# Moving every input and output buffer of a transpose kernel to a multiple of 256 bytes in its SBUF partition

## The chip, the cores and the metric

The kernel runs on one core of one Trainium2 chip. The metric is the device time in microseconds (us) of one execution. Several executions of each kernel were timed, and the median is quoted with the range. The span is the time from the first to the last instruction of the profiled execution. HBM is the memory outside the core, SBUF the core's own buffer memory, cut into 128 partitions, and PSUM the memory into which TensorE writes.

## The reference

```python
# x: 8192 x 8192 float32
def reference(x):
    return np.transpose(x)
```

The kernel has to read 268 MB from HBM, transpose, and write 268 MB back.

## The kernel before

The kernel works in blocks of 1024 rows by 2048 columns. Two loads bring a block into an input buffer. TensorE transposes it in tiles of 128 by 128 against an identity matrix, ScalarE and VectorE take turns in copying the results from PSUM into output buffers, and each full output buffer is stored. There are 64 loads of 4 MB and 128 stores of 2 MB.

```python
    R = 8
    C = 16
    I = R * P            # 1024
    J = C * P            # 2048
    G = 4
    LS = 2

    const_pool = ctx.enter_context(tc.tile_pool(name="const", bufs=1))
    in_pool = ctx.enter_context(tc.tile_pool(name="in_pool", bufs=2))
    out_pool = ctx.enter_context(tc.tile_pool(name="out_pool", bufs=4))
    # ... psum pool
    ident = const_pool.tile([P, P], dt)
    make_identity(nc, ident)
    # ... for each block:
            in_tile = in_pool.tile([P, R, J], dt)
            rs = R // LS
            for s in range(LS):
                src = x[i0 + s * rs * P:i0 + (s + 1) * rs * P, j0:j0 + J]
                src = src.rearrange("(a p) j -> p a j", p=P)
                nc.sync.dma_start(out=in_tile[:, s * rs:(s + 1) * rs, :], in_=src)
            for g in range(C // G):
                out_tile = out_pool.tile([P, G, I], dt)
                # ... transposes into PSUM, copies into out_tile
                dst = out[j0 + g * G * P:j0 + (g + 1) * G * P, i0:i0 + I]
                dst = dst.rearrange("(b q) i -> q b i", q=P)
                nc.scalar.dma_start(out=dst, in_=out_tile)
```

The contiguous runs are 8192 bytes for a load (`J` floats) and 4096 bytes for a store (`I` floats). Each is one DMA packet. The pools are laid out one after another in a partition. In the built program 16 KB of scratch, 128 bytes of constants and the 512-byte identity come first, so the input buffers start at bytes 17024 and 82560 and the output buffers from 148096 on. All of these are 128 past a multiple of 256. The sizes of the buffers are multiples of 256, so every packet in them starts at 128 past one as well.

## Time and profile before

| | before |
|---|---|
| time, median (range) | 1279.2 us (1277.5 to 1279.7) |
| DMA rate over the span | 421 GB/s |
| TensorE, VectorE, ScalarE busy | 55%, 25%, 20% |

These lines are from the page of the kernel before. The first gives busy time per engine with its share of the span. The next two cut the span in 40 slices: busy tenths of the 16 DMA engines, and the rate. Then come the two data queues, stores (q10) and loads (q1), with packets, MB, and the time that their packets took as a share of 16 engines' span. The last is the chain of work that ended last.

```profile
PE 700.7 (55%) x4096; PEld 629.0 (49%) x4096; DVE 313.5 (25%) x256; ACT 252.8 (20%) x257; POOL 0.7 (0%) x6
...
DMA  9999999999999999999999999999999999999999
GB/s 392 425 423 424 425 423 425 423 422 424 423 422 423 424 424 423 424 422 423 424 424 422 422 422 424 424 423 423 423 423 424 422 422 422 424 424 423 422 422 375
...
q10 hardware_dynamic: 67584, 268.44, 51.4%
q1 hardware_dynamic: 33792, 268.44, 49.8%
...
DMA out_dram<-out_tile 87%; PE ps L63 6%; DVE out_tile L71 3%; DMA in_tile<-in_x_dram 2%; ACT out_tile L69 0%; DVEq L71 0%; ACTq L69 0%; SPq L55 0%
```

No compute engine is near full. The DMA engines are busy from the first slice to the last, and the rate is flat. The chain is stores for 87% of the span. The kernel is bound by DMA, so what a packet costs should move its time.

Two stretches of the same trace, from the view of busy time by window. The columns are: window and length in us, then busy us (and instructions) of PE, PEld, DVE, ACT and POOL, the clock granted to TensorE, the DMA share and the rate in GB/s. In the first window only loads run; in the second both directions do, apart from short pauses of the loads.

```profile
14.00:28.00 14.00, 7.81 (x40) 7.40 (x39) 2.45 (x2) 2.06 (x3) 0.00 (x0) 0.76 1.02 424
...
100.00:600.00 500.00, 277.85 (x1600) 249.21 (x1600) 122.14 (x101) 97.72 (x100) 0.00 (x0) 0.73 1.02 423
```

The trace also has a record of every DMA packet. 31618 of 32768 load packets last exactly 309 ns, and 64265 of 65536 store packets exactly 159 ns.

### The profile page before, as it was taken

Reading aid. Unit: us, or ns where it says so; the run is one execution under the profiler, and the core shown is the slowest. Engines: PE = TensorE matmul, PEld = TensorE weight load, DVE = VectorE, ACT = ScalarE, POOL = GpSimd, SP = SyncE. Lnnn points to the kernel's source line nnn. Section 1 sums busy time; section 2 is a strip of 40 time slices with the busy share of each in tenths; the row PEclk is TensorE's granted clock in tenths of the full one; section 3 lists DMA queues with packets and bytes.
Section 4 is the critical chain, followed back from the end, with each engine's and each line's share of the span. In section 5 each row is a group of like instructions: output and inputs, shape, how many; then the busy total and the mean of one; then the engine's idle time right before and its main releaser. Section 6 shows DMA issues by size and latency. Waiting matters only on the chain.

```text
span 1276.3 us, 9511 instructions
## 1 busy us (share of the span) xinstructions
PE 700.7 (55%) x4096; PEld 629.0 (49%) x4096; DVE 313.5 (25%) x256; ACT 252.8 (20%) x257; POOL 0.7 (0%) x6
## 2 busy tenths in 40 slices
PE   3555555655565545655556555555555655556463
PEld 3454455544554544544445554454444544445453
DVE  1222223222232222322123221222222322122222
ACT  1221112121121211212112121221211212112121
POOL 0000000000000000000000000000000000000000
PEclk8777777767777677776677766878667777677867
DMA  9999999999999999999999999999999999999999
GB/s 392 425 423 424 425 423 425 423 422 424 423 422 423 424 424 423 424 422 423 424 424 422 422 422 424 424 423 423 423 423 424 422 422 422 424 424 423 422 422 375
DMA packets 101418, 537.49 MB, mean 421 GB/s; under 512 B 3072, under 2 KB 3072, under 8 KB 68608
## 3 DMA queue, kind: packets, MB, share of 16 engines
q10 hardware_dynamic: 67584, 268.44, 51.4%
q1 hardware_dynamic: 33792, 268.44, 49.8%
q8 instruction: 32, 0.52, 0.1%
q14 instruction: 10, 0.08, 0.0%
HBM read 268.44 MB, written 268.44 MB: 421 GB/s over the span
## 4 chain that ended last, share of the span: by engine, by line
DMA 89%; PE 6%; DVE 3%; issue 0%; ACT 0%; DVEq 0%; ACTq 0%; SPq 0%
DMA out_dram<-out_tile 87%; PE ps L63 6%; DVE out_tile L71 3%; DMA in_tile<-in_x_dram 2%; ACT out_tile L69 0%; DVEq L71 0%; ACTq L69 0%; SPq L55 0%
## 5 line engine op out<-in xcount | busy, mean ns | idle before, releaser
L63 PE MATMUL ps<-ident,in_tile 128*128 128x128 f32 x4096 | 700.7, 344 | 560.5 <-DVE out_tile L71 535.3
L63 PEld LDWEIGHTS ps<-ident,in_tile 128*128 128x128 f32 x4096 | 629.0, 181 | 631.9 <-DVE out_tile L71 605.9
L71 DVE COPY out_tile<-ps 128x1024 f32<-128x1024 f32 x256 | 313.5, 1225 | 948.9 <-DMA out_dram<-out_tile 593.7
L69 ACT COPY out_tile<-ps 128x1024 f32<-128x1024 f32 x256 | 251.5, 1014 | 1007.1 <-DMA out_dram<-out_tile 832.2
L69 ACT ACT_TABLE_LOAD x1 | 1.3, 1283 | 0.7 <-PEq L91 0.7
masks.py:199 POOL TENSOR_SCALAR_AFFINE_SELECT ident<-ident 128x128 f32<-128x128 f32 x1 | 0.3, 292 | 0.1
masks.py:197 POOL MEMSET ident<- 128x128 f32 x1 | 0.2, 204 | 0.3 <-POOLq L91 0.3
L91 POOL MEMSET const-bfloat16-1.0<- 128x1 bf16 x1 | 0.1, 101 | 0.0
L91 POOL MEMSET const-uint8-127<- 128x1 uint8 x1 | 0.1, 101 | 0.0
L91 POOL MEMSET const-float32-0.0<- 128x1 f32 x1 | 0.1, 98 | 0.2 <-issue 0.2
L91 POOL MEMSET const-float32-1.0<- 128x1 f32 x1 | 0.1, 98 | 0.0
## 6 DMA issues: line engine op xcount, KB each, us to landing
in_tile<-in_x_dram SPq DMA_DIRECT2D x64, 4096.0 KB, 27.9
out_dram<-out_tile ACTq DMA_DIRECT2D x128, 2048.0 KB, 28.9
```

The lines of the kernel that those rows point to most:

```text
L63: nc.tensor.transpose(ps[:, a * P:(a + 1) * P], in_tile[:, a, b * P:(b + 1) * P], ident,)
L69: nc.scalar.copy(out=out_tile[:, bb, :], in_=ps)
L71: nc.vector.tensor_copy(out=out_tile[:, bb, :], in_=ps)
L91: nc = _bacc.Bacc("TRN2", target_bir_lowering=False, num_devices=1)
```

## The change

The intent is that every DMA packet begins at a multiple of 256 bytes in its partition. A tile of 128 bytes is put in front of the identity. The buffers then start at 17152, 82688, 148224 and so on, which are all multiples of 256.

```diff
+    pad = const_pool.tile([P, 32], dt)
+    nc.gpsimd.memset(pad, 0.0)
     ident = const_pool.tile([P, P], dt)
     make_identity(nc, ident)
```

Nothing else changes. The instruction streams of all engines are the same in order, but for one more memset on GpSimd.

## The prediction

> **What bounds the kernel now.** The 16 DMA engines. In the 40-slice view they are 90% busy or more throughout and move 422 to 425 GB/s in every slice but the first and last; 537 MB at 421 GB/s over the span. TensorE is busy 55%, VectorE 25%, ScalarE 20%. The chain that ended last is 89% DMA, nearly all stores. Their waits for stores (594 and 832 us) stand behind full queues. Only what makes a DMA packet cheaper moves the time.
>
> **What the change does.** Built, the buffers before start at byte 17024 (input) and 148096 (output) of a partition, all at 128 past a multiple of 256. The 128-byte pad puts all on a multiple. Packets stay 8 KB (loads) and 4 KB (stores), HBM addresses stay. Instruction order is the same but for one more GpSimd memset; the one on the identity took 0.2 us, long before the first load lands at about 13 us. It costs nothing.
>
> **What it could be worth.** The Trainium skill, "DMA: Bandwidth & Descriptors", section "How a descriptor splits into AXI transactions", says that a transaction starts at a multiple of 256 bytes and unused bytes before the start still cost 32-byte beats: here 4, so 132 for 128 in a store, and 260 for 256 in a load if writes pay too. Estimates:
> - both sides pay, exposed: 12 beats of 524 per load packet and two store packets, 2.3%: about 1250 us;
> - only reads (stores) pay: 8 of 520: about 1260 us;
> - hidden behind a fixed cost per packet but for one cycle: about 1271 us;
> - not exposed: 1279 us.
>
> **What the trace says of it.** Nearly all load packets of 8192 bytes last 309 ns, store packets of 4096 bytes 159 ns: 150 ns per 4096 bytes plus a constant 9 ns. The 4-byte semaphore packets, no buffer data, last 9 ns too. Instruction fetches of 8192 bytes, which don't touch these buffers, also last 309 ns while the queues are busy. So the constant looks like a cost of any packet, equal in both directions, and not the price of the start. In even flow packets follow each other about 3 ns closer than they last (DMA shares of 101 to 102%): about 306 and 155.5 ns, 4 beats over bare data. Either account explains that; but the page's read-side rule would not have loads pay as much as stores. Its "Why small descriptors are slow" names a fixed overhead of about 3 cycles per packet, close to this.
>
> **Prediction.** Mostly no effect: **1276 us**, 1256 to 1283 in 8 of 10 cases. Chances: faster by over 2% 0.12, within 2% 0.87, slower 0.01.
>
> **What would show each step.**
> - Right: packets keep 309 and 159 ns, mid-span slices 422 to 425 GB/s.
> - Start matters on both sides: slices at 431 to 434 GB/s, packets near 304 and 154 ns, the span 28 us shorter, evenly over the slices.
> - Only reads pay: store packets shorter, load packets still 309 ns, slices at 429 to 430 GB/s, about 19 us.
> - Engine times per instruction stay in any case (VectorE copy 1225 ns).
>
> **What would make it wrong.** A packet's recorded length may not include its fetch, so that the 9 ns says nothing of the start; or instruction fetches may be unaligned too. Then the gain is 19 to 28 us. A loss would need a cost of the new start (256 past a multiple of 512); nothing in the trace suggests one.

## The result, and the profile after

| | before | after |
|---|---|---|
| time, median (range) | 1279.2 us (1277.5 to 1279.7), 4 runs | 1276.7 us (1276.6 to 1277.0), 4 runs |
| ratio after / before | | 0.9983, 95% interval 0.9969 to 0.9997 |

A ratio is the mean time of one kernel's fast runs over that of the other's fast runs of the same rounds, so it is not quite the ratio of the two medians. The change is worth 2.5 us, or 0.2%. That is inside the forecast range and 0.7 us from the 1276 us that was named.

The same lines of the page of the changed kernel:

```profile
PE 699.8 (55%) x4096; PEld 629.3 (49%) x4096; DVE 313.4 (25%) x256; ACT 253.3 (20%) x257; POOL 0.8 (0%) x7
...
DMA  9999999999999999999999999999999999999998
GB/s 393 425 423 424 425 425 424 424 423 425 425 424 423 424 424 424 425 424 424 424 425 425 423 425 424 425 424 424 423 425 425 424 423 424 423 424 425 424 423 353
...
q10 hardware_dynamic: 67584, 268.44, 51.2%
q1 hardware_dynamic: 33792, 268.44, 49.8%
...
DMA out_dram<-out_tile 80%; PE ps L67 11%; DVE out_tile L75 6%; DMA in_tile<-in_x_dram 2%; ACT out_tile L73 0%; DVEq L75 0%; SPq L59 0%; ACTq L73 0%
```

And the same two windows of the changed kernel:

```profile
14.00:28.00 14.00, 7.96 (x40) 7.55 (x39) 2.45 (x2) 2.10 (x3) 0.00 (x0) 0.76 1.01 429
...
100.00:600.00 500.00, 278.33 (x1604) 250.10 (x1604) 122.74 (x101) 98.81 (x101) 0.00 (x0) 0.72 1.02 424
```

Three things are to be seen. The slices still run at 423 to 425 GB/s, not at the 431 to 434 that a start priced in both directions would have brought. The share of the store queue fell from 51.4% to 51.2%, which is 0.2% of 1275 us, about 2.6 us per engine; the load queue's did not move. And where loads run alone, the rate did rise, from 424 to 429 GB/s. That window is so short a part of the span that it is worth little: 14 us at 1.2% are 0.2 us.

The packet records agree. Packets of 309 ns (32290 of them now) and of 159 ns (64590) are as before. What fell is the number of store packets that last over 200 ns: 284 before, 37 after. Summed over what each takes above 159 ns and divided by 16 engines, these long packets cost 3.2 us per engine before and 0.6 us after. This difference of 2.6 us is about the size of the gain in the medians.

It is not simply the gain of these two traces, whose spans differ by 1.3 us (1276.3 and 1275.0). By the bytes in the packet records, the changed kernel is ahead by about 2.8 us at 1200 us, and then gives part of it back at the end, where its stores come less densely. The same window near the end, before and after:

```profile
1240.00:1270.00 30.00, 15.20 (x126) 13.30 (x123) 9.80 (x8) 8.10 (x8) 0.00 (x0) 0.88 1.02 419
```

```profile
1240.00:1270.00 30.00, 15.26 (x111) 13.38 (x109) 9.73 (x8) 7.26 (x8) 0.00 (x0) 0.83 0.98 404
```

### The profile page after: what moved, and what is told of

It reads as the page before. It is cut to its first block, busy times and chain, and to the rows that moved or that the text cites. A ratio compares the mean times of both kernels' runs of the same rounds, so it can differ in the third digit from the quotient of the medians.

```text
span 1275.0 us, 9512 instructions
## 1 busy us (share of the span) xinstructions
PE 699.8 (55%) x4096; PEld 629.3 (49%) x4096; DVE 313.4 (25%) x256; ACT 253.3 (20%) x257; POOL 0.8 (0%) x7
## 3 DMA queue, kind: packets, MB, share of 16 engines
q10 hardware_dynamic: 67584, 268.44, 51.2%
## 4 chain that ended last, share of the span: by engine, by line
DMA 81%; PE 11%; DVE 6%; issue 1%; ACT 0%; DVEq 0%; SPq 0%; ACTq 0%
DMA out_dram<-out_tile 80%; PE ps L67 11%; DVE out_tile L75 6%; DMA in_tile<-in_x_dram 2%; ACT out_tile L73 0%; DVEq L75 0%; SPq L59 0%; ACTq L73 0%
```

## The experiments

Theory F: a packet costs a fixed time beyond its bytes, and the start of a buffer costs nothing. Rival H: the bytes in front of the start are fetched, in beats of 32 bytes as the prediction counts them, but up to about four beats hide under that fixed cost. Rival P: every such beat is paid. The result was already against P in its full form.

The diffs of the kernels below are against the changed kernel, those of the probes and of `r4c32` against the kernel before; those of the probes are shortened.

### The changed kernel again, a control, and two worse starts

Four kernels ran on one chip, five timed rounds each, against nine runs of the kernel before (1278.4 us, 1277.7 to 1279.1).

`a256_again` is the changed kernel unedited.

> The changed kernel once more, beside its controls on one chip. All theories: 1277 us, 0.998 of before, because that was measured. If the 0.2% was the chip's or the hour's, 1.000.

`ctl128` has the memset and a pad, but a pad that leaves all starts at 128:

```diff
-    pad = const_pool.tile([P, 32], dt)
+    pad = const_pool.tile([P, 64], dt)
```

> Control: the pad is 256 bytes and not 128, so there is the same extra memset and the same build, but all buffers start 128 past a multiple of 256 as before. If the small gain of 2.4 us comes from the start of the buffers: 1279 us, ratio 1.000 (and 1.002 over the changed kernel). If it comes from anything else that an extra memset moves: 1277 us, ratio 0.998.

`off224` puts all starts at 224 past a multiple of 256:

```diff
-    pad = const_pool.tile([P, 32], dt)
+    pad = const_pool.tile([P, 24], dt)
```

> The pad is 96 bytes: all buffers start 224 past a multiple of 256, 7 beats of 32 bytes past it, where before had 4. Theory F (a fixed cost per packet, the start costs nothing): 1277 to 1280 us, packets 309 and 159 ns. Rival H (the start's beats are fetched, but up to about 4 of them hide under the fixed cost of a packet): 3 more beats for each of 4096 store packets per engine show, 14 us, or 22 us if loads pay too: 1293 to 1301 us, store packets at about 163 ns. Rival P (every beat before the start is paid in full) is already hit by the result, and would have 1300 us as well.

`off4` puts them at 4 bytes past one:

```diff
-            in_tile = in_pool.tile([P, R, J], dt)
+            in_raw = in_pool.tile([P, R * J + 64], dt)
+            in_tile = in_raw[:, 1:1 + R * J].rearrange("p (r j) -> p r j", r=R)
-                out_tile = out_pool.tile([P, G, I], dt)
+                out_raw = out_pool.tile([P, G * I + 64], dt)
+                out_tile = out_raw[:, 1:1 + G * I].rearrange("p (g i) -> p g i", g=G)
```

> The buffers start 4 bytes past a multiple of 256 (one float), so that no 32-byte beat of SBUF holds the same bytes as a beat of HBM. Theory F: 1277 to 1280 us. Rival H: 1 extra beat, hidden: the same. If what counts is the beat of 32 bytes and not the block of 256, one more beat per packet, at most 7 us: 1286 us, packets one ns longer. Anything above 1290 us would be a cost that no theory here has.

| start past a multiple of 256 | kernel | time, median (range) | ratio (95%) |
|---|---|---|---|
| 0 | a256_again | 1276.7 us (1276.5 to 1277.1) | 0.9987 (0.9974 to 1.0001) |
| 128 | ctl128 | 1277.6 us (1276.4 to 1278.6) | 0.9995 (0.9983 to 1.0008) |
| 224 | off224 | 1279.2 us (1277.2 to 1281.3) | 1.0008 (0.9995 to 1.0020) |
| 4 | off4 | 1279.7 us (1279.3 to 1280.1) | 1.0011 (0.9998 to 1.0024) |

Rivals H and P had 1293 to 1301 us for `off224`; it took 1279.2. From the best start to the worst the kernel moves by 3 us in 1277. F holds for the kernel as a whole. Still, there is a small order in the table, and it is the same in the packet records of these four (table below); but all four intervals contain 1, so the times alone do not establish it. The control is inconclusive by its times alone: it lies between before and after, and its range overlaps both.

### DMA alone, one direction at a time

`probe_starts` computes nothing. Its output is wrong, which doesn't matter for the time. It issues transfers of 4 MB on one queue, six for each stretch, with the start and the packet as the variables (each stretch also has HBM rows of its own):

```diff
-    (the transpose)
+    for start, run in ((0, 2048), (32, 2048), (56, 2048), (1, 2048), (0, 1024), (0, 512)):
+        ... six loads of 4 MB into raws[n % 6][:, start:start + W], packets of `run` floats
+    for start, run in ((0, 1024), (32, 1024), (56, 1024), (1, 1024), (0, 2048), (0, 512)):
+        ... six stores of 4 MB from there, each to its own part of the output
```

> Wrong result on purpose: no compute, DMA alone on one queue, in 12 stretches of 6 transfers of 4 MB: loads in 8 KB packets to starts at 0, 128, 224 and 4 past a multiple of 256, then loads of 4 KB and 2 KB packets at 0; then stores in 4 KB packets from starts at 0, 128, 224 and 4, then of 8 KB and 2 KB at 0. Theory F: loads at the same rate at all four starts (428 GB/s, packets 309 ns), stores too (421 GB/s, packets 159 ns). Rival H: stores at 224 about 411 GB/s, the other starts alike. Rival P: 0 best, 435 GB/s, 224 worst. By F a packet costs about 5 ns beyond its bytes, so 2 KB packets run at about 408 GB/s, 4 KB at 421, 8 KB at 428, in both directions, and last about 84, 159 and 309 ns.

The view of windows for this probe, one window inside each stretch. The columns are window, length, DVE and POOL busy, clock, DMA share, GB/s. The first four are loads at starts 0, 128, 224 and 4; the sixth is loads in 2 KB packets; the four after it are stores at 0, 128, 224 and 4; the last is stores in 2 KB packets.

```profile
15.00:64.00 49.00, 10.01 (x2) 6.60 (x1) 1.00 1.01 428
75.00:123.00 48.00, 0.00 (x0) 0.00 (x0) 1.00 1.01 422
135.00:183.00 48.00, 0.00 (x0) 0.00 (x0) 1.00 1.01 421
195.00:243.00 48.00, 0.00 (x0) 0.00 (x0) 1.00 1.01 419
...
315.00:364.00 49.00, 0.00 (x0) 0.00 (x0) 1.00 1.04 383
380.00:427.00 47.00, 0.00 (x0) 0.00 (x0) 1.00 1.02 422
440.00:486.00 46.00, 0.00 (x0) 0.00 (x0) 1.00 1.02 422
500.00:548.00 48.00, 0.00 (x0) 0.00 (x0) 1.00 1.02 404
562.00:610.00 48.00, 0.00 (x0) 0.00 (x0) 1.00 1.01 406
...
682.00:740.00 58.00, 0.00 (x0) 0.00 (x0) 1.00 1.06 364
```

This was a miss for F: with one direction at a time, the start does cost. Loads lose 1.4% to 2.1%, and stores at 224 and 4 lose 4%. It was no hit for the rivals by beats either: a start at 4 costs as much as one at 224, and stores at 128 cost nothing here. The packets of 2 KB, 4 KB and 8 KB mostly last 84, 159 and 309 ns, as F said, but the 2 KB ones run at 383 and 364 GB/s, well under the 408 expected.

The order of the stretches might have made this, so `probe_order` turns it round, with an aligned stretch in the midst and at the end.

```diff
-    (loads, then stores, as above)
+    for start in (56, 1, 32, 0, 56, 0):   # stores, 4 KB packets
+    for start in (1, 56, 32, 0, 32, 0):   # loads, 8 KB packets
```

> Wrong result on purpose: DMA alone, one direction at a time, stretches of 6 transfers of 4 MB, the order of the first such probe turned round. Stores of 4 KB packets from starts 224, 4, 128, 0, 224, 0 past a multiple of 256, then loads of 8 KB packets to starts 4, 224, 128, 0, 128, 0. If the start of the buffer made the first probe's slow stretches: stores at 224 and 4 about 405 GB/s and at 128 and 0 about 421 wherever they stand in the order; loads about 419 at 4, 421 at 224, 422 at 128 and 428 at 0. If the place in the order or the rows of the output made them: the third and fourth stretch of stores slow, at about 405 GB/s, whatever their start (here 128 and 0), the first two at 421; and loads 428 in the first stretch, 419 to 422 later.

The same view of this second probe. Stores at 224, 4, 128, 0; then 224 in an early and a late window; then 0. After them loads at 4, 224, 128, 0, 128, 0.

```profile
15.00:66.00 51.00, 10.01 (x2) 6.60 (x1) 1.00 1.02 405
76.00:128.00 52.00, 0.00 (x0) 0.00 (x0) 1.00 1.01 406
138.00:190.00 52.00, 0.00 (x0) 0.00 (x0) 1.00 1.02 406
200.00:250.00 50.00, 0.00 (x0) 0.00 (x0) 1.00 1.02 422
260.00:280.00 20.00, 0.00 (x0) 0.00 (x0) 1.00 1.02 422
296.00:312.00 16.00, 0.00 (x0) 0.00 (x0) 1.00 1.02 407
322.00:370.00 48.00, 0.00 (x0) 0.00 (x0) 1.00 1.02 422
382.00:430.00 48.00, 0.00 (x0) 0.00 (x0) 1.00 1.01 420
442.00:490.00 48.00, 0.00 (x0) 0.00 (x0) 1.00 1.01 421
502.00:550.00 48.00, 0.00 (x0) 0.00 (x0) 1.00 1.01 422
562.00:608.00 46.00, 0.00 (x0) 0.00 (x0) 1.00 1.01 429
622.00:668.00 46.00, 0.00 (x0) 0.00 (x0) 1.00 1.01 423
680.00:727.00 47.00, 0.00 (x0) 0.00 (x0) 1.00 1.01 428
```

The start is what counts, not the place in the order: 0 is at full rate wherever it stands (one trace of each probe). But the price is not a fixed sum per packet. Stores at 224 after an aligned stretch begin at 422 GB/s and fall to 407 some 25 us later in the same stretch, while at the head of this probe they ran at 405 from the first window on; stores at 128 ran at 422 after an aligned stretch in the first probe and at 406 after a slow one in the second. In these probes a stream off a multiple of 256 could run at full rate and then drop out of it; the aligned ones, with packets of 4 or 8 KB, stayed there. What drops it is not shown.

### DMA alone, both directions

Why, then, does the kernel not pay? In it, loads and stores run together. `probe_mix` does that without compute:

```diff
-    (loads, then stores, as above)
+    for start in (32, 0, 56, 0, 1):
+        for k in range(12):
+            ... nc.sync.dma_start(4 MB load, 8 KB packets, into raws[n % 6][:, start:start + W])
+            ... nc.scalar.dma_start(4 MB store, 4 KB packets, from the same)
```

> Wrong result on purpose: DMA alone, loads (8 KB packets) and stores (4 KB packets) together in a ring of six 4 MB buffers, in five stretches of 12 loads and 12 stores at starts 128, 0, 224, 0 and 4 past a multiple of 256. If the load's price of a start off 256 is hidden when the engines also store (rival H as the load stretches of the first probe leave it): 423 to 424 GB/s in all five, at most 1 GB/s apart, as in the kernels. If mixing does not hide it and the kernel hides it by its waits: 424 at 0 and about 420 or less at 128, 224 and 4.

The view of windows of this probe (columns: window, length, POOL busy, clock, DMA share, GB/s), each window where both directions have the same start: 128, 0, 224, 0, 4.

```profile
40.00:180.00 140.00, 0.00 (x0) 1.00 1.02 425
300.00:420.00 120.00, 0.00 (x0) 1.00 1.02 425
540.00:655.00 115.00, 0.00 (x0) 1.00 1.02 425
775.00:890.00 115.00, 0.00 (x0) 1.00 1.02 425
1015.00:1130.00 115.00, 0.00 (x0) 1.00 1.02 424
```

In a steady mix the start costs nothing that shows. Of its 61440 store packets all but 19 last exactly 159 ns, in the stretches off 256 just as in the aligned ones. So the price of a start does not appear while the other direction runs too, and no number of beats decides it. Whether the other direction hides the price, or keeps the stream from dropping out, is not shown.

The mix alone does not explain the kernel. In each of the eight traces of its versions with 8 KB loads the loads pause 29 times, for about 9 us at a time and 250 to 264 us in all, a fifth of the span; then stores run alone. By the packet records they moved 421 GB/s in these pauses at every start, aligned or not. So pauses this short did not bring the price either.

### Which of the two buffers matters

The kernel still gains a little: 2.5 us when first measured, 1.7 us in the second measurement (`a256_again`, 1276.7 against 1278.4 us). The long store packets in the trace of the kernel before come in groups of about ten, some 40 us apart, once per block. Each group sits where loads begin again after about 9 us in which only stores ran, because the loads had waited for the input buffer (in the kernel before loads pause from 249.0 to 258.3 us on the clock of the packet records, which begins 10.5 us before the span, and 11 long store packets follow at 258 us). In the changed kernel the pauses are about as long (9.1 us and 8.5 us in the median) and the groups are gone: within 3 us of the loads' return there are 251 long store packets before and 2 after. Most of the 37 that are left have another occasion: 32 of them overlap an instruction fetch of 16 KB (queue q8), as do 28 to 31 in each of the other traces, whatever the start. Two kernels make one part of the change each.

`in128` (output aligned, input at 128 as before):

```diff
-            in_tile = in_pool.tile([P, R, J], dt)
+            in_raw = in_pool.tile([P, R * J + 64], dt)
+            in_tile = in_raw[:, 32:32 + R * J].rearrange("p (r j) -> p r j", r=R)
```

> One part of the change alone: output buffers start at multiples of 256, input buffers 128 past one as before. In the traces so far the only steady difference is in store packets of over 200 ns: 284 in before, 223 to 312 at starts of 128, 224 and 4, but 37 and 38 in the changed kernel; they come when loads begin again after some 9 us with stores alone, and cost 2.5 us per engine. If they come from the loads' writes into buffers off a multiple of 256: 200 to 300 such packets, about 1278 us. If from the stores' reads: about 40 and 1276.7 us. The first 28 us, loads alone, run at 422 to 424 GB/s here in either case.

`out128` (input aligned, output at 128 as before):

```diff
-                out_tile = out_pool.tile([P, G, I], dt)
+                out_raw = out_pool.tile([P, G * I + 64], dt)
+                out_tile = out_raw[:, 32:32 + G * I].rearrange("p (g i) -> p g i", g=G)
```

> The other part alone: input buffers start at multiples of 256, output buffers 128 past one. If the long store packets come from the stores' reads: 200 to 300 of them, about 1279 us. If from the loads' writes: about 40, and 1276.7 us. The first 28 us, loads alone, run at 428 GB/s in either case.

Against nine runs of before (1278.2 us), `in128` took 1276.9 us (1276.6 to 1277.2; ratio 0.9989) and `out128` 1277.9 us (1276.5 to 1279.5; ratio 0.9999). The store queue's line and the window with loads alone, first for `in128`:

```profile
q10 hardware_dynamic: 67584, 268.44, 51.2%
```

```profile
14.00:28.00 14.00, 7.79 (x37) 7.38 (x36) 2.45 (x2) 2.02 (x2) 0.00 (x0) 1.00 1.01 422
```

then for `out128`:

```profile
q10 hardware_dynamic: 67584, 268.44, 51.4%
```

```profile
14.00:28.00 14.00, 7.97 (x48) 7.51 (x48) 2.58 (x3) 3.03 (x3) 0.00 (x0) 1.00 1.01 427
```

The two effects come apart. The rate of loads alone follows the input buffers; the share of the store queue follows the output buffers. The counts of the packet records, one trace per kernel:

| input, output start | kernel | store packets over 200 ns | their excess, us per engine | median us |
|---|---|---|---|---|
| 128, 128 | before | 284 | 3.2 | 1279.2 |
| 128, 128 | ctl128 | 223 | 2.5 | 1277.6 |
| 224, 224 | off224 | 257 | 2.7 | 1279.2 |
| 4, 4 | off4 | 312 | 3.2 | 1279.7 |
| 0, 128 | out128 | 261 | 2.8 | 1277.9 |
| 128, 0 | in128 | 35 | 0.6 | 1276.9 |
| 0, 0 | after | 37 | 0.6 | 1276.7 |
| 0, 0 | a256_again | 38 | 0.6 | 1276.7 |

The counts part cleanly by the output's start. So does the rate, by the bytes in the packet records: in the first microsecond after the loads return it is 388 to 400 GB/s in the five traces with output buffers off 256 and 425 in the three with aligned ones; from 100 to 1200 us it is 422.5 to 422.9 against 423.6 to 423.7. That difference of about 0.2% is 2 to 3 us of these 1100. The medians come from three batches of runs, in which before had 1279.2, 1278.4 and 1278.2 us. The times go the same way, but single kernels (`ctl128`, `out128`) spread over 2 to 3 us and can't be told from either side by time alone. No version beat the changed kernel; `in128` equals it.

### What a packet costs

If a packet has a fixed cost, then another cut of the same bytes must show it. `r4c32` keeps the starts at 128 and the sizes of all transfers, but has 16 KB load packets and 2 KB store packets:

```diff
-    R = 8
-    C = 16
+    R = 4
+    C = 32
-    G = 4
+    G = 8
```

> Starts as before (128), but the block is 4 by 32 tiles and not 8 by 16: the same bytes and number of transfers, 16 KB load packets and 2 KB store packets, so per engine 1024 and 8192 packets and not 2048 and 4096: 3072 more. Theory F (about 5 ns a packet beyond its bytes): 15 us slower, about 1294 us, ratio 1.011. If the gap to the bare rate were no cost per packet (only a lower clock of the fabric): 1279 us.

It took 1322.2 us (1322.0 to 1324.2), ratio 1.035. From its page:

```profile
GB/s 399 412 400 415 407 408 411 405 413 411 407 411 404 410 413 408 409 408 413 410 408 415 404 399 416 410 413 404 410 407 408 411 407 406 414 411 408 406 408 344
...
q10 hardware_dynamic: 133120, 268.44, 54.0%
q1 hardware_dynamic: 17408, 268.44, 48.2%
```

The direction is F's, the size is not: 44 us, not 15. The usual lengths fit the fixed cost: 84 ns for 2 KB stands on one line with 159 and 309 (150 ns per 4096 bytes, and 9 ns more), and 611 ns for 16 KB is 2 ns above it. But the mean lengths are 86.9 and 620.6 ns. Per engine that is 8192 x 2.9 + 1024 x 9.6 = 33 us of stalls, where before had 5 (4096 x 0.9 + 2048 x 0.8). The additional 28 us and the 15 us forecast make 43 of the 44 measured, if stalls on different queues do not overlap. Of the 33 us, 23 are in the 2 KB store packets and 10 in the 16 KB load packets, so both sides stall more than before; the forecast left that out. That the packet's size makes these stalls is not shown: `r4c32` also walks HBM and PSUM in another order.

## Why the prediction was right or wrong

- **The bound was right.** The DMA engines set the time, but for the end of the span; the memset of 0.1 us and the instruction streams did not count.
- **"Packets keep 309 and 159 ns" was right**, and so was the main inference from it. In the mixed flow that fills most of the span the constant 9 ns belongs to the packet and not to the start: the changed kernel's packets still last 309 and 159 ns, and the mixed probe ran at 424 to 425 GB/s at starts of 0, 4, 128 and 224.
- **"Equal in both directions, and not the price of the start" was right only for the mix.** With one direction alone, a start off 256 costs loads 1.4% to 2.1% and can cost stores 4%, though not in the kernel's own pauses of 9 us. The prediction read its packet lengths in a trace where loads run alone for the first 30 us only, and took them for a law of all flows. It had even the counterexample at hand: the window of loads alone in before ran at 424 and not at 428, and I did not read it as a price.
- **The list of outcomes by beats (1250, 1260, 1271, 1279 us) did not hold the true one.** None of the accounts by beats fits: 4 bytes cost as much as 224. The gain came from a place the prediction did not name, namely store packets that stall when loads begin again. With output buffers on a multiple of 256, 2 of 251 are left there. "Mostly no effect" was earned by the packet lengths; that 1276 us was met within 0.7 us is luck, as it stood between outcomes none of which was the true one.
- **The chance of over 2% (0.12)** stood for rival P. The start at 224 (1279.2 us for a forecast of 1293 to 1301) rules it out for this kernel.

Left open: why a stream off 256 can run at full rate and later fall, why a store packet stalls when loads resume almost only if its buffer is off 256, and where the extra stalls of 2 KB and 16 KB packets come from.

## What to carry to other kernels

Start DMA buffers at multiples of 256 bytes: here it cost one memset of 0.1 us. In the probes, stretches of some 60 us with loads alone had 1.4% to 2.1% to win by it, and stretches with stores alone up to 4%. A kernel like this one, with loads and stores together and pauses of about 9 us, had 0.2% to win. So first read from the packet records how much of the span runs in one direction, and for how long at a time. And before taking a rule's cost at face value, look whether the packet lengths in the trace have room for it, in each kind of flow on its own.

## What the Trainium skill lacked or had wrong

- "DMA: Bandwidth & Descriptors", section "How a descriptor splits into AXI transactions": the cost in beats of a start off 256 does not show as such. In mixed flow none is seen (424 to 425 GB/s at starts 0, 4, 128 and 224). In one direction, a start at 4 (419 or 420 GB/s loads, 406 stores) costs as much as one at 224 (421 loads, 404 to 407 stores), and stores at 128 ran at 422 once and 406 once. The page says nothing of writes into SBUF, which also pay: 428 to 422 for loads at 128.
- The same page, section "Why small descriptors are slow", has a fixed overhead of about 3 cycles per packet. The trace agrees that there is one: recorded lengths are 9 ns plus 150 ns per 4096 bytes from 2 KB to 8 KB (609 by that line for 16 KB, where 611 was recorded). Lacking are the stalls on top of it: 2 KB packets ran at 364 to 383 GB/s alone, and `r4c32`, with 2 KB stores and 16 KB loads, lost an estimated 28 us more than before to stalls, beside 15 us of fixed cost.
- The same page, in "Specifications", gives about 358 GB/s as the HBM limit of a core. That row does not bound a core that runs alone, which the page's own measurement of 425 GB/s for loads shows too. Here one core moved 428 GB/s with loads alone and 421 GB/s over a whole span of loads and stores. What the row leaves out, and the page says further down, is that it is the share of a core while both cores of a pair are active.
- "SBUF — State Buffer", section "Operand start alignment", says that its runs timed nothing. Here starts at 4 bytes past a multiple of 256 gave a correct result and cost nothing clear of noise (ratio 1.0011, 95% interval 0.9998 to 1.0024).
